# Opening of a hybrid mLSTM and pooling step: x transposed token tile by token tile, and four adaLN steps one chunk later

## The chip, the core and the metric

One core of a Trainium2 chip runs the kernel as one launch. The metric is the device time in microseconds, lower is better. The engines are TensorE (PE in the profile, with its weight loads as PEld), VectorE (DVE), ScalarE (ACT), GpSimd (POOL) and SyncE (SP), which here only issues transfers. Each engine works through its own list of instructions in order and waits on semaphores for the others. Every tile is float32.

## What is computed

One layer of a backbone over 384 tokens: 128 context tokens and 256 latent tokens, 2048 features each. Cut to what the opening works on:

```python
mod = jax.nn.silu(cond) @ ada_w + ada_b            # cond: c_ctx for the context, c for the latents
shift_a, scale_a, ... = mod reshaped to 6 x 2048
h = _rmsnorm(x, norm_w[0]) * (1 + scale_a) + shift_a
proj = h @ w_in                                    # q, k, v, o, gates, u
```

Behind that come a bidirectional mLSTM over q, k, v and a pooling mixer over u, one output projection, and an MLP of width 8192. They make up most of the time, and the change does not touch them.

## The kernel before, in words

Products are taken in three passes: each operand is split into a rounded high part (`hi`, made by ACT) and a remainder (`lo`, made by DVE), and PE adds hi·hi, hi·lo and lo·hi (line 503 for the stage at hand). Weights arrive in tiles named `raw_u`, `raw_v` and so on, which `load_w` (lines 122 to 142) loads through SP's queue and splits; three `raw` buffers go round.

The opening has these parts.

- **x.** The three token tiles `xtok` (128 tokens by 2048 features, 1 MB each) are loaded on SP's queue behind the two condition vectors `cc` and the constants `cst` (identity, ones, a selection matrix). ACT squares each tile and sums by token (line 389), and DVE and POOL make the reciprocal root `rx`. PE spreads it over all partitions (`bc_rx`), and DVE copies that to `rbc`.
- **Transposes.** The projections need the features on the partitions. `transpose_x(k)` takes one block of 128 features, transposes it for all three token tiles into one PSUM bank (line 403), and copies the 384 columns to `xT[k]`, on DVE for even k and on ACT for odd k (lines 409 to 411). So it needs all three tiles. The table `X_ORDER` orders the first eight blocks: "t" is one block, "a" one step of the adaLN generator, "b" the copy to `rbc`. Four more blocks come in `shift_rows`, between the two halves of `make_h(0)`, and the last four after the first weight chunk (`XT_AT`).
- **adaLN.** The modulation of two feature blocks (k-step of 256 features) at a time: PE multiplies the silu of both condition vectors by slabs `ada_raw` of ada_w (128x4x256, 512 KB, line 257), ACT copies the sum (`ada_sb`), PE turns it by small matmuls (line 273), and DVE adds the bias into `mod`. `first_ada` is a generator: each `next` does one slab or one later part. For features 0 to 255 it has two runs of four slabs (scale, then shift), ten steps in all. For features 256 to 511 it has eight slabs in a row, with the shift's four and then the scale's four; four buffers go round, so that the second four slabs may be loaded only when PE has read the first four. From features 512 on, `ada_eight` loads eight slabs at once, four of them into buffers that are free at the time (upper halves of the `u` tiles, which share memory with `xtok`, and part of `masks`; line 366).
- **The projection of u and v** (lines 491 to 526). Eight k-steps s, each with five weight chunks: u with 512 columns, u with 512, v with 3, 3 and 2 heads (the last with the gate columns). `make_h(s)` makes the modulated features `hm`, `hh`, `hl`. For s = 0, `ADA_STEPS` says how many adaLN steps PE does behind each chunk: four behind chunk 0 and four behind chunk 2. They are the eight slabs of features 256 to 511.

The order of PE, DVE and ACT is written by hand up to `order.close()` (line 488). From there PE's order is by hand up to the end of this loop; the other engines' lists, and SP's, are set by a scheduler.

Of the kernel before, what the change touches and what calls it, by code (L numbers as in the profile page):

```python
# [7 lines left out]
F32 = mybir.dt.float32  # L8
F32R = mybir.dt.float32r
AF = mybir.ActivationFunctionType  # L10
ALU = mybir.AluOpType
AX = mybir.AxisListType

P = 128
D = 2048
KT = D // P
NTOK = 384
# [10 lines left out]
N_W = 4  # L28
N_ADA = 4
N_E = 1  # L30
XT_AT = 0
ADA_STEPS = (4, 0, 4, 0, 0)
X_ORDER = "tatatatattaatabata"
N_X = 4
RATE_GF = 0.4
RATE_GS = 0.25
# [2 lines left out]
N_AHEAD = 3  # L39
# [5 lines left out]
def hymba_kernel(  # L45
# [6 lines left out]
    nc = tc.nc  # L52
    w_in, w_out, w1, w2, ada_w = w_in[0], w_out[0], w1[0], w2[0], ada_w[0]

    const = ctx.enter_context(tc.tile_pool(name="const", bufs=1))
    wp = ctx.enter_context(tc.tile_pool(name="wp", bufs=3))
# [4 lines left out]
    dram = ctx.enter_context(tc.tile_pool(name="dram", bufs=1, space=bass.MemoryType.DRAM))  # L61

    def slot(name, dt=F32):
        return slots.tile([P, 386], dt, tag="t", name=name)

    def bank(name):
        return psum.tile([P, 512], F32, tag="ps", name=name)


    cst = const.tile([P, 3, P], F32, name="cst")  # L70
    cs_src = consts.rearrange("p (n q) -> p n q", q=P)
    ident = cst[:, C_ID, :]
    ones = cst[:, C_ONE, :]
    cc = const.tile([P, 2, 16], F32, name="cc")
    vp_scope, pre_scope = ExitStack(), ExitStack()
    vp = vp_scope.enter_context(tc.tile_pool(name="vp", bufs=1))
    pre = pre_scope.enter_context(tc.tile_pool(name="pre", bufs=1))
    prm = pre.tile([P, 2, P], F32, name="prm")
    masks = vp.tile([P, N_CST - 3, P], F32, name="masks")
    nc.sync.dma_start(cc[:, 0, :], c_ctx.rearrange("(p j) -> p j", j=16))  # L80
    nc.sync.dma_start(cc[:, 1, :], c[0].rearrange("(p j) -> p j", j=16))
    nc.sync.dma_start(cst[:, 0:3], cs_src[:, 0:3])

    vsb = [vp.tile([P, NH, 129], F32, name=f"v{i}") for i in range(3)]
    gsb = vp.tile([P, 3, 32], F32, name="gsb")
    x_tok = [pre.tile([P, D], F32, tag=f"x{i}", name=f"xtok{i}") for i in range(3)]
    for t, src in zip(x_tok, (x_prompt[0], x_sample[0, 0:128], x_sample[0, 128:256])):
        nc.sync.dma_start(t, src)
    nc.gpsimd.dma_start(prm[0:96, 1, :], ada_b[0].rearrange("(r p) -> r p", p=P))
    nc.gpsimd.dma_start(prm[0:64, 0, :], norm_w[0].rearrange("i (k p) -> (i k) p", p=P))  # L90
    nc.gpsimd.dma_start(prm[64:72, 0, :], mlstm_norm_w[0].rearrange("(k p) -> k p", p=P))
# [106 lines left out]
    def rstd_cols(out, ss, n, scale):  # L198

        nc.vector.tensor_scalar(out, ss, scale, EPS, op0=ALU.mult, op1=ALU.add)  # L200
        nc.gpsimd.tensor_tensor(out, out, mhalf[:, 0:n], op=ALU.pow)
# [143 lines left out]
    def first_ada():  # L345
        for k0, nk in ksteps:
            if k0 == 0:
                yield from ada_mat([(1, k0, nk)])
                yield from ada_mat([(0, k0, nk)], ("lo",))
            elif k0 == 2:  # L350
                yield from ada_mat([(0, k0, nk), (1, k0, nk)])
            else:
                yield from ada_eight(k0)
# [21 lines left out]
        yield from ada_rows([(0, k0, 2), (1, k0, 2)], ps)  # L375

    ada0 = first_ada()
    pp = bank("pp")
    nc.tensor.transpose(pp[:, 0:96], prm[0:96, 1, :], ident[0:96, 0:96])
    nc.tensor.transpose(pp[:, 96:176], prm[0:80, 0, :], ident[0:80, 0:80])  # L380
    nc.vector.tensor_copy(prmT[:, 80:176], pp[:, 0:96])
    nc.vector.tensor_copy(prmT[:, 0:80], pp[:, 96:176])

    ssq = const.tile([P, 3, 2], F32, name="ssq")
    junk = wp.tile([P, 1024], F32, tag="hi", name="junk", bufs=N_W)
    rx = const.tile([P, 3], F32, name="rx")
    for i in (0, 1, 2):
        for q in range(2):
            nc.scalar.activation(junk, x_tok[i][:, q * 1024:(q + 1) * 1024], AF.Square, accum_out=ssq[:, i, q:q + 1])

    xT_dram = dram.tile([P, KT, NTOK], F32, name="xT_dram")
    xT = []
    rbc = pre.tile([P, NTOK], F32, name="rbc")
    ss = const.tile([P, 3], F32, name="ss")
    nc.vector.tensor_reduce(ss, ssq, axis=AX.X, op=ALU.add)
    rstd_cols(rx, ss, 3, 1.0 / D)

    xt_late = []

    def transpose_x(k, later=False):  # L400
        ps = bank(f"xt_{k}")
        for i in range(3):
            nc.tensor.transpose(ps[:, i * P:(i + 1) * P], x_tok[i][:, k * P:(k + 1) * P], ident)
        t = slot(f"xT{k}")
        xT.append(t)

        def copy():
            if k % 2:
                nc.scalar.activation(t[:, 0:NTOK], ps[:, 0:NTOK], AF.Copy)
            else:  # L410
                nc.vector.tensor_copy(t[:, 0:NTOK], ps[:, 0:NTOK])

        if later:
            xt_late.append(copy)
        else:
            copy()

    for op in X_ORDER:
        if op == "t":
            transpose_x(len(xT))  # L420
        elif op == "a":
            next(ada0)
        else:
            nc.vector.tensor_copy(rbc, bcast_row(rx, "rx")[:, 0:NTOK])
# [12 lines left out]
    def make_h(s, between=None):  # L437
        ts = []
        for k in range(ksteps[s][0], sum(ksteps[s])):
            t, hi, lo = slot(f"hm{k}"), slot(f"hh{k}", F32R), slot(f"hl{k}", F32R)  # L440
            ts.append((k, t, hi, lo))
            for g, (a, b) in enumerate(GROUPS):
                nc.vector.scalar_tensor_tensor(t[:, a:b], xT[k][:, a:b], mod[:, 1, k, g:g + 1], rbc[:, a:b], op0=ALU.mult, op1=ALU.mult)
        if between is not None:
            between()
        for k, t, hi, lo in ts:
            for g, (a, b) in enumerate(GROUPS):
                i1 = nc.scalar.activation(hi[:, a:b], t[:, a:b], AF.Identity, bias=mod[:, 0, k, g:g + 1])
                i2 = nc.vector.scalar_tensor_tensor(lo[:, a:b], t[:, a:b], mod[:, 0, k, g:g + 1], hi[:, a:b].bitcast(F32), op0=ALU.add, op1=ALU.subtract)
            h.append((hi, lo))  # L450
        return i1.ins, i2.ins
# [16 lines left out]
    def load_ahead(m, n):  # L468
        for q in range(m, min(m + n, NS * len(chunks))):
            if q not in loaded:  # L470
                s, ci = divmod(q, len(chunks))
                loaded[q] = load_chunk(s, ci, h_ins if s == 0 else ())
                if q == NS * len(chunks) - 1:
                    with tc.issue_after(load_w.ins):
                        nc.sync.dma_start(masks, cs_src[:, 3:N_CST])

    def shift_rows():
        for _ in range(2):
            transpose_x(len(xT), True)
        next(ada0)  # L480
        for _ in range(2):
            transpose_x(len(xT), True)

    h_ins = make_h(0, shift_rows)
    lo_later[0]()
    for copy in xt_late:
        copy()
    order.close()
    order2 = ExitStack()
    order2.enter_context(tc.manual_schedule(engines={mybir.EngineType.PE}))  # L490
    for s in range(NS):
        for ci, (kind, c0, w) in enumerate(chunks):
            k0, nk = ksteps[s]
            load_ahead(5 * s + ci, 1 if s + ci == 0 else N_AHEAD)
            hi, lo, n = loaded.pop(5 * s + ci)
            acc = [bank(f"{kind}_{c0}_{s}_{i}") for i in range(3)]

            ways = ((0, 0), (1, 0), (0, 1))
            for ps in [ways[n:n + 1] for n in range(3)] if s == ci == 0 else [ways]:
                for k in range(nk):  # L500
                    for i in range(3):
                        for a, b in ps:
                            nc.tensor.matmul(acc[i][:, 0:n], h[k0 + k][a][:, i * P:(i + 1) * P], (hi, lo)[b][:, k, :],  # L503
                                             start=k == 0 and a + b == 0, stop=k == nk - 1 and b == 1)
                    if ci == 3 and k == 0:
                        next(ada0, None)
            if s == ci == 0:
                load_ahead(1, 1)
            if s == 0 and ci == XT_AT:
                while len(xT) < KT:  # L510
                    transpose_x(len(xT))
            for _ in range((ADA_STEPS if s == 0 else (1, 1, 1, 0, 0))[ci]):
                next(ada0, None)
            if ci == 3 and s < NS - 1:
                make_h(s + 1)
            for i in range(3):
                if kind == "u":
                    dst, src = u_sb[i][:, c0:c0 + w], acc[i][:, 0:n]
                else:
                    dst, src = vsb[i][:, c0:c0 + w, 0:128], acc[i][:, 0:w * P].rearrange("p (h e) -> p h e", e=P)  # L520
                if s == 0:
                    nc.scalar.activation(dst, src, AF.Copy)
                else:
                    nc.vector.tensor_tensor(dst, src, dst, op=ALU.add)
                if kind == "v" and c0 == 6:
                    nc.vector.tensor_tensor(gsb[:, i, :], acc[i][:, w * P:n], gbias if s == 0 else gsb[:, i, :], op=ALU.add)
# [326 lines left out]
    ps = bank("ps_nout")  # L853
# [43 lines left out]
    for cols in ([0, 256], [512], [768], [1024], [1280], [1536], [1792]):  # L897
        if cols[0] in (768, 1024, 1280):
            for m in range(2):
                n = len(early)  # L900
                t = y[n // 2][:, 1024 * (n % 2):1024 * (n % 2) + 1024].rearrange("p (j c) -> p j c", c=256)
# [495 lines left out]
```

## Time and profile before

| | |
|---|---|
| Time, median of 3 runs | 1684.31 us (1683.07 to 1687.94) |
| Profiled execution, its own time | 1684.17 us |
| Its span from the first to the last instruction | 1682.5 us |
| Instructions | 27870 |
| Bytes moved by DMA | 320.95 MB, mean 191 GB/s |

Times in the profile count from the span's start. A row of the timeline gives start and length in us, engine, line, operation, tile written and tiles read, and in brackets the idle time ahead of it and what ended that. A row of the chain of waits gives start, length and what the chain went through. A row of the DMA view gives tiles, issuing queue, count, size and the median time from the start of the issue to landing. In a row of windows the last three numbers are the granted clock, the busy share of the DMA engines and GB/s.

### The profile page before, as it was taken

The numbers are of one execution on the slowest core, as the hardware profiler recorded it, in microseconds if no ns is written. First come the engines' busy times: TensorE is split into PE (matmuls) and PEld (weight loads), VectorE is DVE, ScalarE is ACT, GpSimd is POOL, SyncE is SP. The second block draws the span as 40 slices with busy tenths as digits, with TensorE's granted clock in tenths as the row PEclk, the third lists the DMA queues.
The fourth block names the chain that finished last, engine by engine and source line by source line (L and its number), as shares of the span: only waits on it lengthen the run. The fifth ranks groups of instructions, "written<-read, shape, count | busy, mean of one in ns | idle before, by whom it ended". The sixth has DMA issues, their size and how long they took to land.

```text
span 1682.5 us, 27870 instructions
## 1 busy us (share of the span) xinstructions
PE 1654.3 (98%) x10965; PEld 1581.4 (94%) x10965; DVE 1340.3 (80%) x2009; ACT 751.3 (45%) x1225; POOL 133.3 (8%) x185
## 2 busy tenths in 40 slices
PE   6999999999999999999999999999999999999997
PEld 3888999999999989989999999999999999999996
DVE  3677769898999959997897688988588588588688
ACT  5322355555443345543444444444444444445443
POOL 1000002221000024520000000000000000000120
PEclk9999999999999999999999999999999999999999
DMA  9999757786789954754546246444344443443653
GB/s 318 332 310 298 253 172 248 240 258 221 238 273 311 311 194 142 209 151 128 178 154 195 84 135 187 152 144 150 101 151 129 123 138 118 145 124 113 186 182 136
DMA packets 258099, 320.95 MB, mean 191 GB/s; under 512 B 14784, under 2 KB 223120, under 8 KB 257584
## 3 DMA queue, kind: packets, MB, share of 16 engines
q1 hardware_dynamic: 250688, 303.62, 57.1%
q0 software_dynamic: 5984, 13.78, 2.9%
q8 instruction: 86, 1.41, 0.4%
q10 hardware_dynamic: 1296, 1.77, 0.3%
q14 instruction: 45, 0.37, 0.1%
HBM read 308.61 MB, written 10.51 MB: 190 GB/s over the span
## 4 chain that ended last, share of the span: by engine, by line
PE 94%; DVE 3%; issue 1%; DMA 1%; ACT 0%; SPq 0%; POOL 0%; DVEq 0%; ACTq 0%; POOLq 0%
PE acc_w L145 10%; PE acc_w L144 10%; PE acc_w L146 10%; PE v L503 4%; PE y L1231 4%; PE y L1232 4%; PE y L1230 4%; PE u L503 4%; PE acc_wo L144 3%; PE acc_wo L145 3%; PE acc_wo L146 2%; PE y_yz L1231 2%; PE y_yz L1230 2%; PE y_yz L1232 2%; PE y L1074 2%; PE y L1073 2%
## 5 line engine op out<-in xcount | busy, mean ns | idle before, releaser
L145 PE MATMUL acc_w<-h2l,hi_w 128*128 128x384 f32 (+1 forms) x1024 | 346.2, 338 | 0.5 <-DVE h2l L1024 0.5
L144 PE MATMUL acc_w<-h2h,hi_w 128*128 128x384 f32 (+1 forms) x1024 | 344.2, 338 | 1.2 <-ACT h2h L1020 1.2
L146 PE MATMUL acc_w<-h2h,lo_w 128*128 128x384 f32 (+1 forms) x1024 | 345.1, 337 | 0.0
L136 DVE TENSOR_TENSOR lo_w<-raw_w,hi_w 128x1024 fp32r<-128x1024 f32 x152 | 185.3, 1220 | 136.5 <-ACT hi_w L135 136.3
L135 ACT ACTIVATE hi_w<-raw_w 128x1024 fp32r<-128x1024 f32 x152 | 160.8, 1058 | 213.7 <-PE acc_w L145 83.4
L317 DVE SCALAR_TENSOR_TENSOR ada_acc<-ada_raw,sg,ada_acc 128x1024 f32<-128x1024 f32 (+1 forms) x240 | 252.0, 1081 | 2.1 <-DMA ada_raw<-in_ada_w_dram 2.1
L144 PEld LDWEIGHTS acc_w<-h2h,hi_w 128*128 128x128 f32 x1024 | 192.2, 188 | 2.9 <-ACT h2h L1020 2.0
L145 PEld LDWEIGHTS acc_w<-h2l,hi_w 128*128 128x128 f32 x1024 | 192.6, 188 | 1.2 <-DVE h2l L1024 0.8
L146 PEld LDWEIGHTS acc_w<-h2h,lo_w 128*128 128x128 f32 x1024 | 192.4, 188 | 0.3 <-DVE lo_w L136 0.2
L1216 ACT ACTIVATE hi_t<-w 128x1024 fp32r<-128x1024 f32 x104 | 109.5, 1059 | 118.7 <-PE y L1232 34.0
L1217 DVE TENSOR_TENSOR lo_t<-w,hi_t 128x1024 fp32r<-128x1024 f32 x104 | 126.3, 1220 | 15.1 <-ACT hi_t L1216 14.7
L1217 DVE TENSOR_TENSOR lo_b<-w,hi_b 128x1024 fp32r<-128x1024 f32 x78 | 95.3, 1221 | 40.0 <-ACT hi_b L1216 39.8
L1216 ACT ACTIVATE hi_b<-w 128x1024 fp32r<-128x1024 f32 x78 | 82.5, 1060 | 97.0 <-PE acc_w L145 64.6
L135 ACT ACTIVATE hi_wo<-raw_wo 128x1024 fp32r<-128x1024 f32 x32 | 34.0, 1064 | 81.3 <-DMA raw_wo<-in_w_out_dram 64.0
L950 ACT ACTIVATE z<-acc_w 128x384 f32<-128x384 f32 x54 | 26.3, 487 | 74.8 <-PE acc_w L146 74.8
L503 PE MATMUL v<-hi_v,hh 128*128 128x384 f32 (+1 forms) x144 | 47.8, 332 | 0.0
L503 PE MATMUL v<-lo_v,hh 128*128 128x384 f32 (+1 forms) x144 | 46.5, 323 | 0.0
L503 PE MATMUL v<-hi_v,hl 128*128 128x384 f32 (+1 forms) x144 | 46.5, 323 | 0.0
L136 DVE TENSOR_TENSOR lo_wo<-raw_wo,hi_wo 128x1024 fp32r<-128x1024 f32 x32 | 38.8, 1218 | 7.3 <-ACT hi_wo L135 6.3
L986 POOL DMA_DIRECT2D gf_dram<-gfT x1 | 0.5, 521 | 551.9 <-DVE gfT L985 551.9
L144 PE MATMUL acc_k<-hh,hi_k 128*128 128x384 f32 x128 | 44.2, 345 | 0.0
L144 PE MATMUL acc_o<-hh,hi_o 128*128 128x384 f32 x128 | 43.9, 343 | 0.0
(2268 smaller groups left out, 4566.9 us busy)
## 6 DMA issues: line engine op xcount, KB each, us to landing
raw_w<-in_w_dram SPq DMA_DIRECT2D x152, 512.0 KB, 4.3
ada_raw<-in_ada_w_dram SPq DMA_DIRECT2D x130, 512.0 KB, 5.0
w<-in_w_dram SPq DMA_DIRECT2D x104, 512.0 KB, 4.4
raw_wo<-in_w_out_dram SPq DMA_DIRECT2D x32, 512.0 KB, 5.6
u<-in_ada_w_dram SPq DMA_DIRECT2D x18, 512.0 KB, 6.0
raw_u<-in_w_in_dram SPq DMA_DIRECT2D x16, 512.0 KB, 7.0
raw_q<-in_w_in_dram SPq DMA_DIRECT2D x16, 512.0 KB, 4.7
raw_k<-in_w_in_dram SPq DMA_DIRECT2D x16, 512.0 KB, 4.7
```

The lines of the kernel that those rows point to most:

```text
L135: nc.scalar.activation(hi[:, 0:n], raw[:, 0:n], AF.Copy)
L136: low = lambda: nc.vector.tensor_tensor(lo[:, 0:n], raw[:, 0:n], hi[:, 0:n].bitcast(F32), op=ALU.subtract)
L144: nc.tensor.matmul(ps, lh, rh, start=start, stop=False)
L145: nc.tensor.matmul(ps, lh, rl, start=False, stop=False)
L146: mm3.ins = nc.tensor.matmul(ps, ll, rh, start=False, stop=stop).ins
L317: nc.vector.scalar_tensor_tensor(acc[:, g, :], raw[:, a, :], cj, acc[:, g, :], op0=ALU.mult, op1=ALU.add)
L503: nc.tensor.matmul(acc[i][:, 0:n], h[k0 + k][a][:, i * P:(i + 1) * P], (hi, lo)[b][:, k, :], start=k == 0 and a + b == 0, stop=k == nk - 1 ...
L1216: nc.scalar.activation(hi, raw, AF.Copy)
L1217: nc.vector.tensor_tensor(lo, raw, hi.bitcast(F32), op=ALU.subtract)
L1230: nc.tensor.matmul(acc, xh, wh, start=start and j == 0, stop=False)
L1231: nc.tensor.matmul(acc, xh, wl, start=False, stop=False)
L1232: nc.tensor.matmul(acc, xl, wh, start=False, stop=stop and j == 3)
```

## The change

The three x tiles are transposed one after the other. Each has four PSUM banks of four blocks, and every block of 128 columns is copied on its own into its third of `xT[k]`; the last bank of the first tile and the last two banks of the third are copied by ACT, all others by DVE. All 48 transposes stand ahead of the first adaLN slab. The squares of a tile stand ahead of its transposes. The first x tile is the first transfer of SP's queue, `cc` follows, and `cst` goes out on ACT's queue. The eight adaLN steps of the first k-step stand four behind chunk 1 and four behind chunk 2, and the weights are loaded one chunk ahead for chunks 0 and 1.

```diff
-XT_AT = 0
-ADA_STEPS = (4, 0, 4, 0, 0)
-X_ORDER = "tatatatattaatabata"
+ADA_STEPS = (0, 4, 4, 0, 0)
+X_ORDER = "aaabaaaaaa"
...
-    nc.sync.dma_start(cc[:, 0, :], c_ctx.rearrange("(p j) -> p j", j=16))
-    nc.sync.dma_start(cc[:, 1, :], c[0].rearrange("(p j) -> p j", j=16))
-    nc.sync.dma_start(cst[:, 0:3], cs_src[:, 0:3])
+    nc.scalar.dma_start(cst[:, 0:3], cs_src[:, 0:3])
...
-    for t, src in zip(x_tok, (x_prompt[0], x_sample[0, 0:128], x_sample[0, 128:256])):
-        nc.sync.dma_start(t, src)
+    nc.sync.dma_start(x_tok[0], x_prompt[0])
+    nc.sync.dma_start(cc[:, 0, :], c_ctx.rearrange("(p j) -> p j", j=16))
+    nc.sync.dma_start(cc[:, 1, :], c[0].rearrange("(p j) -> p j", j=16))
+    for i in (1, 2):
+        nc.sync.dma_start(x_tok[i], x_sample[0, (i - 1) * P:i * P])
...
+    def transpose_x(i, k0, on_act):
+        ps = bank(f"xt_{i}_{k0}")
+        for a in range(4):
+            nc.tensor.transpose(ps[:, a * P:(a + 1) * P], x_tok[i][:, (k0 + a) * P:(k0 + a + 1) * P], ident)
+        for a in range(4):
+            dst, src = xT[k0 + a][:, i * P:(i + 1) * P], ps[:, a * P:(a + 1) * P]
+            if on_act:
+                nc.scalar.activation(dst, src, AF.Copy)
+            else:
+                nc.vector.tensor_copy(dst, src)
+
+    squares(0)
+    for q in range(4):
+        transpose_x(0, 4 * q, q == 3)
...
+    squares(1)
+    for q in range(4):
+        transpose_x(1, 4 * q, False)
+    squares(2)
+    for q in range(4):
+        if q == 2:
+            nc.vector.tensor_reduce(ss, ssq, axis=AX.X, op=ALU.add)
+            rstd_cols(rx, ss, 3, 1.0 / D)
+        transpose_x(2, 4 * q, q >= 2)
...
-    h_ins = make_h(0, shift_rows)
+    h_ins = make_h(0, lambda: next(ada0))
     lo_later[0]()
-    for copy in xt_late:
-        copy()
...
-            load_ahead(5 * s + ci, 1 if s + ci == 0 else N_AHEAD)
+            load_ahead(5 * s + ci, 1 if s == 0 and ci < 2 else N_AHEAD)
...
-            if s == 0 and ci == XT_AT:
-                while len(xT) < KT:
-                    transpose_x(len(xT))
```

The lists below give line, operation, tile written, tiles read, and the shape; "x4" is four in a row. The first is PE's list before, where u's chunk 0 (`u_0_0` to `u_0_2` with `hi_u_0_258`, `lo_u_0_259`) ends and chunk 1 (`hi_u_0_333`) begins:

```order
L503 MATMUL u_0_1_311<-lo_u_0_259,hh_267 128x512
L503 MATMUL u_0_2_312<-lo_u_0_259,hh_267 128x512
L403 MATMUL xt_337<-cst,xtok_89 128x128
...
L403 MATMUL xt_355<-cst,xtok_91 128x128
L257 MATMUL ada_2_361<-ada_raw_2_0_362,cT 32x256 x4
L257 MATMUL ada_2_361<-ada_raw_2_4_368,cT 32x256 x4
L257 MATMUL ada_2_361<-ada_raw_2_8_374,cT 32x256 x4
L257 MATMUL ada_2_361<-ada_raw_2_12_380,cT 32x256 x4
L503 MATMUL u_0_0_401<-hi_u_0_333,hh_262 128x512
```

Now PE's list from the end of chunk 1 (`hi_u_0_385`, `lo_u_0_386`) to v's first chunk (`hi_v_0_443`), and from its end to the second set of slabs:

```order
L493 MATMUL u_0_2_394<-lo_u_0_386,hh_343 128x512
L257 MATMUL ada_2_413<-ada_raw_2_0_414,cT 32x256 x4
L257 MATMUL ada_2_413<-ada_raw_2_4_420,cT 32x256 x4
L257 MATMUL ada_2_413<-ada_raw_2_8_426,cT 32x256 x4
L257 MATMUL ada_2_413<-ada_raw_2_12_432,cT 32x256 x4
L493 MATMUL v_0_0_460<-hi_v_0_443,hh_338 128x384
...
L493 MATMUL v_0_2_462<-lo_v_0_444,hh_343 128x384
L257 MATMUL ada_2_413<-ada_raw_2_0_481,cT 32x256 x4
L257 MATMUL ada_2_413<-ada_raw_2_4_487,cT 32x256 x4
L257 MATMUL ada_2_413<-ada_raw_2_8_493,cT 32x256 x4
L257 MATMUL ada_2_413<-ada_raw_2_12_499,cT 32x256 x4
```

The twelve transposes are gone from this place, the first set of slabs has moved behind chunk 1, and only v's first chunk is left between the two sets; before, chunk 1 and v's first chunk stood there.

SP's list now, from the last pieces of v's weights of the first k-step to the weights of the second (`u_326` is the spare half of a u tile):

```order
L129 DMA raw_v_0_453<-in_w_in_dram 128x2x256
L129 DMA raw_v_0_453<-in_w_in_dram 128x2x32
L366 DMA u_326<-in_ada_w_dram 128x4x256
L253 DMA ada_raw_2_0_481<-in_ada_w_dram 128x4x256
L253 DMA ada_raw_2_4_487<-in_ada_w_dram 128x4x256
L253 DMA ada_raw_2_8_493<-in_ada_w_dram 128x4x256
L253 DMA ada_raw_2_12_499<-in_ada_w_dram 128x4x256
L129 DMA raw_u_1_510<-in_w_in_dram 128x2x512
L129 DMA raw_u_1_563<-in_w_in_dram 128x2x512
```

The load of `u_326` is new at this place: before, it stood behind the weights `raw_u_1` and the next `raw_v`, and the second set of slabs followed the `raw_v_0` pieces directly. Apart from this one and the first rows, where `xtok` now precedes `cc` and `cst` is gone, SP's list has the same order as before.

More of the change, by code (lines that the diff above doesn't have):

```diff
@@ L377, in hymba_kernel, with squares @@
     ada0 = first_ada()
+    ssq = const.tile([P, 3, 2], F32, name="ssq")
+    junk = wp.tile([P, 1024], F32, tag="hi", name="junk", bufs=N_W)
+    rx = const.tile([P, 3], F32, name="rx")
+    ss = const.tile([P, 3], F32, name="ss")
+    xT_dram = dram.tile([P, KT, NTOK], F32, name="xT_dram")
+    xT = [slot(f"xT{k}") for k in range(KT)]
+    rbc = pre.tile([P, NTOK], F32, name="rbc")
+    def squares(i):
+        for q in range(2):
+            nc.scalar.activation(junk, x_tok[i][:, q * 1024:(q + 1) * 1024], AF.Square, accum_out=ssq[:, i, q:q + 1])
+    def transpose_x(i, k0, on_act):
[11 more added lines that the diff above has]
+        transpose_x(0, 4 * q, q == 3)
     pp = bank("pp")
@@ L382, in hymba_kernel @@
     nc.vector.tensor_copy(prmT[:, 0:80], pp[:, 96:176])
[L384 to L415, printed above, removed]
-            copy()
+    squares(1)
[7 more added lines that the diff above has]
+        transpose_x(2, 4 * q, q >= 2)
     for op in X_ORDER:
-        if op == "t":
-            transpose_x(len(xT))
-        elif op == "a":
+        if op == "a":
             next(ada0)
@@ L475, in load_ahead @@
                         nc.sync.dma_start(masks, cs_src[:, 3:N_CST])
[L477 to L482, printed above, removed]
-    h_ins = make_h(0, shift_rows)
+    h_ins = make_h(0, lambda: next(ada0))
     lo_later[0]()
-    for copy in xt_late:
-        copy()
     order.close()
@@ L508, in hymba_kernel @@
                 load_ahead(1, 1)
-            if s == 0 and ci == XT_AT:
-                while len(xT) < KT:
-                    transpose_x(len(xT))
             for _ in range((ADA_STEPS if s == 0 else (1, 1, 1, 0, 0))[ci]):
```

## The prediction

> **What bounds the kernel now.** I read the page's busy shares first, then TensorE's waits from 30 us to the end, then the chain of the opening, then the transfers that the chain rests on.
>
> ```profile
> PE 1654.3 (98%) x10965; PEld 1581.4 (94%) x10965; DVE 1340.3 (80%) x2009; ACT 751.3 (45%) x1225; POOL 133.3 (8%) x185
> PE   6999999999999999999999999999999999999997
> PE acc_w L144 <- ACT h2h L1020: 1.2, 2, 0.7
> ```
>
> TensorE (PE) is busy 98% of the span, and only the first of the 40 slices is far from full. The last row is the largest of the six entries in PE's waits from 30 us to the end; together they are 3.7 us in 1650. So PE's own work sets the end from 30 us on. A change of the opening is worth the time by which PE gets earlier or later through the first projection weights, and nothing later gives it back or adds to it, unless a new wait appears. The chain of the opening, start, length, what:
>
> ```profile
> 16.32 1.08 PE ada L257 x8
> ...
> 21.50 0.57 PE ada L257 x8
> ...
> 28.03 0.39 ACT ada_sb L269
> 28.42 0.95 ACT hi_u L135
> ...
> 29.39 0.41 ACT hh L448
> ...
> 29.84 4.61 PE u L503 x18
> 34.45 1.31 PE xt L403 x12
> 35.76 1.86 PE ada L257 x32
> 37.62 4.38 PE u L503 x18
> 42.01 3.16 PE v L503 x18
> 45.17 1.87 PE ada L257 x32
> 47.03 1.78 PE v L503 x9
> ```
>
> From 29.84 us PE does, without a gap: u chunk 0, twelve transposes, four adaLN slabs (x32: 2 passes of 16), u chunk 1, v chunk 0, four more slabs, v chunk 1. All seven pieces must be done in any order; I follow the start of v chunk 1, 47.03 us, because behind it PE's list of work is the same in both kernels. Before 29.84 the transfers set the pace. Here each transfer has its issue row and then its row of the DMA view, whose last number is the time from issue to landing:
>
> ```profile
> 0.81 0.38 SPq L80 DMA_DIRECT2D cc<-in_c_ctx_dram  x1
> 2.18 0.43 SPq L88 DMA_DIRECT2D xtok<-in_x_prompt_dram  x1
> xtok<-in_x_prompt_dram SPq DMA_DIRECT2D x1, 1024.0 KB, 5.5
> 17.85 1.42 SPq L253 DMA_DIRECT2D ada_raw<-in_ada_w_dram  x1
> ada_raw<-in_ada_w_dram SPq DMA_DIRECT2D x1, 512.0 KB, 8.9
> 19.31 1.41 SPq L129 DMA_DIRECT2D raw_u<-in_w_in_dram  x1
> raw_u<-in_w_in_dram SPq DMA_DIRECT2D x1, 512.0 KB, 8.8
> 20.00:24.00 4.00, 4.00 (x41) 2.24 (x40) 1.44 (x4) 1.37 (x3) 0.00 (x0) 1.00 1.10 348
> ```
>
> The eighth slab lands at 17.85 + 8.9 = 26.75, the first weights raw_u at 19.31 + 8.8 = 28.1. The queue runs full at 348 GB/s (last row, last column), or 1.51 us for 512 KB. hi_u starts 0.3 us after its data, so the start of u is tied to the transfer stream and not to the transposes.
>
> **The change part by part.** *x first.* The first x tile moves from the fourth place of SP's queue (issue 2.18) to the first (0.81): at most 1.37 us earlier, at least nothing. cst goes to ACT's queue, but its bytes and those of cc still have to be carried, and 208 KB at 348 GB/s are 0.6 us, which leaves 0.8. The queue was not yet full in those first microseconds, so I take 1.0. Then raw_u lands at 27.1, the eighth slab at 25.75; its matmuls (0.57) and copy (0.39) are over by 26.8. From raw_u: hi_u 1.05, and from its end to the first u matmul as before 29.84 - 29.37 = 0.47. u starts at **28.6**, 1.2 earlier.
>
> *Transposes.* All 48 stand ahead of the slabs, while PE waits for transfers. The twelve that stood behind u chunk 0 leave the chain: **1.31** less. A gain of 2.5 us so far. The cover: x's first tile lands near 6.7 (2.18 + 5.5 - 1.0), the first slab near 15.3, and u starts at 28.6. In these 22 us PE has 48 transposes, 5.2 us at 1.31 / 12 or twice that at a slow clock, and eight slabs of 0.57 to 1.08, so 10 to 19 us of work.
>
> *Copies.* Each token tile is copied out in 16 pieces of 128 columns, 48 in all (DVE 36, ACT 12), where there were 16 of 384. None of this shape is in the trace. The nearest:
>
> ```profile
> 9.26 0.26 DVE L381 COPY prmT<-pp 128x96 f32<-128x96 f32 x1 [3.45 <-PE pp L380]
> 20.12 0.56 DVE L411 COPY xT<-xt 128x384 f32<-128x384 f32 x1 [2.16 <-PE xt L403]
> ```
>
> Between 0.26 and 0.56 each; 0.29 by a straight line between the DVE rows, and near the lower one. DVE's eight for the last tile are then 2.3 us, over by about 18, and rx and rbc, which wait behind them, are needed only some 9 us later: nothing on the path. At 0.56 the 36 take 20 us, rbc comes at about 28 and u would start some 2 us later; that is the upper end. The six squares on ACT keep their number, and the issue of cst there (0.4, as on SP) comes ahead of a table load that waits for cc anyway.
>
> *cc behind x.* The silu chain and the clearing of cT were ready near 6 us; behind 1 MB of x they come about 4 us later, still 5 ahead of the first slab. No cost. ACT now splits v's first weights after u chunk 1's second bank instead of ahead of the bank copies; at the 1.05 of hi_u or less it lies under the 1.86 of the first slab set.
>
> *The four slabs one chunk later.* This makes a new wait. The second set of four slabs uses the buffers of the first set, so SP can issue them only as PE reads the first set. Issue and landing before, first and last of the second set:
>
> ```profile
> 36.39 0.37 SPq L253 DMA_DIRECT2D ada_raw<-in_ada_w_dram  x1
> ada_raw<-in_ada_w_dram SPq DMA_DIRECT2D x1, 512.0 KB, 4.0
> 37.95 0.46 SPq L253 DMA_DIRECT2D ada_raw<-in_ada_w_dram  x1
> ada_raw<-in_ada_w_dram SPq DMA_DIRECT2D x1, 512.0 KB, 7.6
> ```
>
> Counted from PE's start on the first set (35.76), the second set lands at +4.6 to +9.8. PE needed its last slab at 45.17 + 3/4 of 1.87 = 46.57, +10.8: one microsecond to spare. u chunk 1, 4.38 us, stood between the two sets and now stands ahead of both. PE reaches the first set at 28.6 + 4.61 + 4.38 = 37.6 and the last slab of the second at 37.6 + 1.86 + 3.16 + 1.40 = 44.0, +6.4. If the second set lands as before, its last slab comes at 37.6 + 9.8 = 47.4 and PE waits 3.4 us; if the four follow each other at 1.51, at 37.6 + 4.6 + 4.5 = 46.7, a wait of 2.7. The queue has drained by then, and one more transfer of 512 KB (for u's spare half) stands in front of the set, so it cannot go ahead of PE. After the last slab (0.47) v chunk 1 starts at 47.2 to 47.9.
>
> *Sum.* 47.03 becomes 47.2 to 47.9: +0.2 to +0.85, I take +0.5. The gain of 2.5 is spent in the new wait. The profiled execution took 1684.17 us, with a span of 1682.5, and 0.14 less than the median of the three runs, 1684.31. The forecast is 1684.17 + 0.5 = **1684.7**.
>
> **The rivals.** *Cold array (slower).* PE had a slow state in the opening that the granted clock (1.00 throughout) doesn't show:
>
> ```profile
> 20.01 1.01 PE L257 MATMUL ada<-ada_raw,cT 128*32 128x256 f32 x8
> 21.43 0.64 PE L257 MATMUL ada<-ada_raw,cT 128*32 128x256 f32 x8
> ```
>
> In the chain the same eight passes cost 1.08 at 16.32 and 0.57 from 21.50 on, after 4 to 5 us without a gap. Before, PE kept busy until u because the transposes filled the gaps between slabs. Now it works 0.57 of every 1.5 us for ten microseconds ahead of u. If that lets it fall back, the eighteen matmuls of u chunk 0 begin slowly: over 4.6 us the loss is 4.6 x (1 - 0.57/1.08) = 2.2 us, and everything behind moves with it: 1686.9. It decides from the share of idle time at which the array slows down. No stretch of this trace has PE fast and then two thirds idle, so the rows speak neither way; as each gap is only about a microsecond, I give it 0.25. [...]
>
> *No new wait.* The second set lands by +6.4 and the gain stays: 1684.17 - 2.5 = 1681.7. Against it: a single slab took 4.0 from issue, and the fourth is issued over 2 us after PE's start. 0.08.
>
> *x is not earlier.* POOL's small transfers or the copies hold the stream, u starts at 29.8: 1685.9. 0.06.
>
> *Late weights of the next k-step.* The raw_u pair of k-step 1 stands behind the second set.
>
> ```profile
> 40.15 0.37 SPq L129 DMA_DIRECT2D raw_u<-in_w_in_dram  x1
> raw_u<-in_w_in_dram SPq DMA_DIRECT2D x1, 512.0 KB, 9.5
> 50.21 1.05 ACT L135 ACTIVATE hi_u<-raw_u 128x1024 fp32r<-128x1024 f32 x1
> 51.53 1.49 ACT L448 ACTIVATE hh<-hm,mod 128x128 fp32r<-128x128 f32 x4
> ```
>
> Its second landed at 49.65, hi_u started 0.56 later, and hh was ready 1.3 ahead of PE's need at 53.2 (47.03 + 1.78 + 0.34 + 4.05): 1.8 us of cover. It should land 1.6 to 1.9 later while PE is 0.2 to 0.85 later, so the cover holds by a few tenths. Each microsecond beyond is one of PE's; two of them give 1686.7, and only some five would pass 0.3%. 0.05.
>
> **How the numbers follow.** Forecast 0.56 (1683.7 to 1685.7), cold array 0.25 (1686 to 1688), no wait 0.08, x not earlier 0.06, late weights 0.05. From 1681.7 to 1688.0 these leave out less than 2 in 10, with the dearest copies inside. 0.3% of this kernel is 5 us, about what a measurement can tell from no change. No case reaches it alone: faster 0.01; slower 0.03, if cold array and late weights come together; within 0.96.
>
> **What would show it.** u's first matmul near 28.6; the chain of 29 to 35 without transposes; an idle stretch of 2.7 to 3.4 us on PE before or among the second four slabs, ended by the ada_raw transfer, in SP's order behind PE's reads; v chunk 1 near 47.5. u chunk 0 taking 6 us or more would show the cold array; a PE wait for hh near 53 the late weights. Wrong altogether if PE has no wait there, or if the span moves by over 4 us.

## The result and the profile after

| | before | after |
|---|---|---|
| Median of 10 runs | 1684.29 us (1683.07 to 1687.94) | 1688.83 us (1687.42 to 1691.79) |
| Ratio after / before, 95% interval | | 1.0027 (1.0017 to 1.0037) |
| Profiled execution, span | 1684.17, 1682.5 us | 1689.48, 1687.8 us |

The change costs 4.5 us, 0.27%, where 0.4 us were forecast. The chain of the kernel after, from the transfer of the first weights on (start, length, what):

```profile
18.69 9.47 DMA raw_u<-in_w_in_dram
...
28.18 1.06 ACT hi_u L135
...
29.59 10.48 PE u L493 x36
40.07 1.91 PE ada L257 x32
...
42.26 7.68 DMA ada_raw<-in_ada_w_dram
...
49.99 0.64 PE ada L257 x8
50.63 3.07 PE v L493 x9
53.69 0.61 PE ada L273 x4
54.30 4.06 PE v L493 x27
58.36 8.36 PE u L493 x36
```

The same pieces stand here as in the chain before, without the transposes. Both u chunks are one row now, 10.48 us instead of 4.61 + 4.38 = 8.99. A transfer stands in the middle of the chain, and behind it `v x9` takes 3.07 us instead of 1.78. u of k-step 1, the last row, begins at 58.36; before it began at 47.03 + 1.78 + 0.34 + 4.05 = 53.2. That is 5.15 us, and PE stays about that much behind until the end (span +5.3).

TensorE's wait for slabs from 25 to 60 us in the kernel after (us in total, times, longest), SP's issue of the second set, and that set on TensorE's timeline (in brackets the idle time ahead and what ended it):

```profile
PE ada L257 <- DMA ada_raw<-in_ada_w_dram: 4.6, 5, 1.1
```

```profile
40.70 2.02 SPq L253 DMA_DIRECT2D ada_raw<-in_ada_w_dram  x4
```

```profile
45.23 0.64 PE L257 MATMUL ada<-ada_raw,cT 128*32 128x256 f32 x8
46.76 0.64 PE L257 MATMUL ada<-ada_raw,cT 128*32 128x256 f32 x8 [0.89 <-DMA ada_raw<-in_ada_w_dram]
48.53 0.64 PE L257 MATMUL ada<-ada_raw,cT 128*32 128x256 f32 x8 [1.14 <-DMA ada_raw<-in_ada_w_dram]
49.99 0.64 PE L257 MATMUL ada<-ada_raw,cT 128*32 128x256 f32 x8 [0.81 <-DMA ada_raw<-in_ada_w_dram]
```

SP issues the set only behind PE's start on the first set (40.07). The last three slabs arrive 1.5 to 1.8 us apart, and the last lands at 42.26 + 7.68 = 49.94, 9.87 behind that start. PE needed it at 45.23 + 1.40 = 46.63 and got it at 49.99, 3.4 us later: 2.8 are the three waits in brackets (the other two of the five lie ahead of u), and the rest is that each slab on its own takes 0.64 us instead of the 0.47 of a slab within four. The load of `u_326`, which stands in front of the set in SP's list, had no part in it: it was issued at 34.37 and landed 5.4 us later, before 40.70.

The slow stretches are in the granted clock. These are windows of the kernel after; the columns used here are the stretch, its length, PE's busy time, and, third from the end, the granted clock:

```profile
19.99:23.40 3.41, 2.72 (x30) 1.07 (x29) 1.41 (x5) 0.38 (x1) 0.00 (x0) 1.00 1.10 348
23.40:26.82 3.42, 1.64 (x24) 0.32 (x16) 0.87 (x3) 0.00 (x0) 0.00 (x0) 1.00 1.07 371
26.82:30.23 3.41, 1.66 (x6) 1.47 (x7) 0.78 (x3) 2.43 (x6) 0.00 (x0) 0.50 1.08 356
30.23:33.64 3.41, 3.41 (x10) 2.67 (x10) 3.18 (x5) 1.34 (x2) 0.00 (x0) 0.50 1.10 349
33.64:37.06 3.42, 3.42 (x16) 2.79 (x15) 0.00 (x0) 1.58 (x3) 0.00 (x0) 1.00 1.02 315
...
47.30:50.71 3.41, 1.46 (x21) 0.47 (x18) 0.00 (x0) 0.02 (x1) 0.00 (x0) 1.00 1.07 379
50.71:54.12 3.41, 3.41 (x13) 3.41 (x13) 0.00 (x0) 1.42 (x2) 0.00 (x0) 0.50 1.07 365
```

Read them in pairs. In 23.40 to 26.82 PE is busy 1.64 of 3.42 us, and the clock of the next window is 0.50. It stays there until a window is full (30.23 to 33.64), and the one behind that is back at 1.00. In 47.30 to 50.71, while PE waits for slabs, it is busy 0.43 of the time, and the next window, with `v x9` in it, is slow. A full window at 0.50 does 1.7 us less work, an estimate (half of 3.41). The bounds aren't chosen here: in this trace every change of the clock falls on this grid of 3.41 us. (Before, the clock read 1.00 even while eight passes cost 1.08 at 16.32; its record begins at 20.83 us, between the slabs of 0.94 at 20.08 and 0.57 at 21.50, so that slow start isn't in it.)

### The profile page after: what moved, and what is told of

It is laid out like the page before. It is cut to its first block, busy times and chain, and to the rows that moved or that the text cites. A ratio compares the mean times of both kernels' runs of the same rounds, so it can differ in the third digit from the quotient of the medians.

```text
span 1687.8 us, 27905 instructions
## 1 busy us (share of the span) xinstructions
PE 1658.9 (98%) x10965; PEld 1587.8 (94%) x10965; DVE 1342.6 (80%) x2037; ACT 749.2 (44%) x1229; POOL 132.1 (8%) x185
## 4 chain that ended last, share of the span: by engine, by line
PE 87%; DVE 6%; DMA 3%; issue 2%; SPq 1%; ACT 1%; POOL 0%; DVEq 0%; ACTq 0%; POOLq 0%
PE acc_w L144 9%; PE acc_w L145 9%; PE acc_w L146 9%; PE v L493 4%; PE u L493 4%; PE y L1218 4%; PE y L1219 4%; PE y L1217 4%; PE acc_wo L144 3%; PE acc_wo L145 2%; PE acc_wo L146 2%; PE y_yz L1218 2%; PE y_yz L1217 2%; PE y_yz L1219 2%; PE y L1059 2%
## 5 line engine op out<-in xcount | busy, mean ns | idle before, releaser
L144 PE MATMUL acc_q<-hh,hi_q 128*128 128x384 f32 x128 | 43.9, 343 | 0.0
```

Source lines behind the costliest of these rows:

```text
L144: nc.tensor.matmul(ps, lh, rh, start=start, stop=False)
```

## The experiments

Times below are medians of 5 to 11 runs, with the ratio to the kernel before on the same chip and its 95% interval. The number to compare in the opening is the start of u of k-step 1: 53.2 before, 58.36 after.

**e1: the steps back.** The kernel after with

```diff
-ADA_STEPS = (0, 4, 4, 0, 0)
+ADA_STEPS = (4, 0, 4, 0, 0)
```

> The kernel after, with the eight adaLN steps at their old places (four behind chunk 0, four behind chunk 2); x, transposes, copies and transfers as in the kernel after. Theory A (the loss comes from the four slabs moved one chunk later: 3.6 us of wait for the second slab set and 1.6 us of a slow array behind it): no wait of PE for ada_raw behind 30 us, `v x9` at 1.8 us instead of 3.07, v chunk 1 at 46.0 to 47.8 instead of 50.63, the time 3.5 to 5 us under the kernel after, within 1 us of the kernel before. u chunk 0 still begins slowly (about 6 us), since the slabs ahead of it come as in the kernel after. Rival B (the loss comes from the transposes and the slow array ahead of u alone): the time stays at least 2.5 us over the kernel before.

1686.07 us, 1.0002 (0.9993 to 1.0011). Its chain:

```profile
29.97 6.77 PE u L493 x18
36.74 1.86 PE ada L257 x32
...
46.15 1.86 PE ada L257 x32
48.02 1.78 PE v L493 x9
...
54.19 8.36 PE u L493 x36
```

The second set has no wait, `v x9` is at full speed, and 4.2 of the 5.15 us are gone. u chunk 0 still takes 6.77 us, more than in the kernel after, since the clock was at 0.50 for three windows here (24.86 to 35.10). v chunk 1, 48.02, is 0.2 later than the theory's bound for that reason.

**e2: the steps alone.** The kernel before with

```diff
-ADA_STEPS = (4, 0, 4, 0, 0)
+ADA_STEPS = (0, 4, 4, 0, 0)
```

> The kernel before, with only the adaLN steps moved (four behind chunk 1, four behind chunk 2); x, transposes, copies and transfers as before. Theory A: PE reaches the first set at 34.45 + 1.31 + 4.38 = 40.1, the second set lands up to +9.9 behind that, at 50.0, v chunk 1 starts near 50.5 and, if gaps of 1 us make the array slow, takes 1.3 us more: the time 3.5 to 5.2 us over the kernel before, as much as the whole change. u chunk 0 stays at 4.6 us. Rival B: no wait or one under 1 us, the time within 1 us of the kernel before.

1691.36 us, 1.0037 (1.0025 to 1.0050): 6.0 us over the kernel before, at least as much as the whole change, where 3.5 to 5.2 were expected. Its chain:

```profile
30.44 4.61 PE u L503 x18
35.05 1.31 PE xt L403 x12
...
40.55 1.91 PE ada L257 x32
...
42.74 9.20 DMA ada_raw<-in_ada_w_dram
...
51.98 1.08 PE ada L257 x8
53.06 3.18 PE v L503 x9
```

u begins at full speed, so the transposes between the slabs did keep the clock up; the last slab lands 11.4 us behind PE's start on the first set, and two slow windows follow the wait (49.78 to 56.60). The 11.4 hold more than the gate: the scheduler changed SP's list too, and here the two loads of `raw_u` for k-step 1 (issued at 36.86 and 39.88) stand in front of the set (41.18). So the wait is shown by e2, but its size isn't that of the moved steps alone. With e1, where the wait goes with the steps, this puts the loss on the moved steps.

**e4 and e5: work for PE in the gaps.** Eight transposes of constants, into a bank that nobody reads, behind each slab of k-step 0 (e4) or behind the first three of the second set of k-step 1 (e5):

```diff
+                fill = 8 if k0 == 0 else 0 if b == 1 and j0 < 12 else 0   # e4
+                fill = 0 if k0 == 0 else 8 if b == 1 and j0 < 12 else 0   # e5
+                if fill:
+                    wps = bank(f"fill_{i}_{k0}_{j0}")
+                for _ in range(fill):
+                    nc.tensor.transpose(wps[:, 0:P], cst[:, C_ONE, :], ident)
```

> The kernel after, with eight transposes of constants added behind each of the first eight slabs, into a bank that nobody reads; the rest as in the kernel after. They fill about 0.9 us of each 1.5 us between slabs. If gaps of about 1 us at 40% load made the array slow ahead of u: u chunks 0 and 1 take 9.0 to 9.3 us instead of 10.48, v chunk 1 comes 1.2 to 1.5 earlier than 50.63, and the time is 1.2 to 1.5 us under the kernel after. If something else slowed u chunk 0 (its operands, the copies of xT, the transfers): u chunks 0 and 1 stay at 10.4.

> The kernel after, with eight transposes of constants added behind each of the first three slabs of the second set of k-step 1, where PE waits for the next slab; the rest as in the kernel after. If the gaps made the array slow there: the wait for the last slab stays (v chunk 1 near 50.6), but `v x9` takes 1.8 us instead of 3.07 and the small matmuls 0.34 instead of 0.61, and the time is about 1.5 us under the kernel after. If the slow v chunk 1 has another cause: `v x9` stays near 3 us and the time that of the kernel after.

The edit also hit a later adaLN stage that runs the same lines (from 612 us on in the kernel before; 32 transposes more in e4, 24 in e5), so their whole times, 1693.56 and 1695.49 us, don't measure the opening. The chains do, e4's row first, then e5's:

```profile
30.85 8.81 PE u L498 x36
```

```profile
50.18 0.57 PE ada L257 x8
50.75 1.78 PE v L498 x9
...
56.93 8.36 PE u L498 x36
```

Both slow stretches went where PE was kept at work, and nothing else was changed: 8.81 instead of 10.48, 1.78 instead of 3.07. Of the gain at u, e4 kept only 0.6 us (u of k-step 1 at 57.75), since its u began 1.3 later: slab and eight transposes take 0.57 + 1.02 us, more than the 1.5 between two slabs.

**e6: both, in the opening alone.**

> The kernel after, with eight transposes of constants (nobody reads them) behind each of the eight slabs of k-step 0 and behind the first three slabs of the second set of k-step 1, and nowhere else in the program. Theory A (the granted clock falls to 0.50 where PE is short of work for some microseconds): clock 1.00 from 18 to 60 us, u chunks 0 and 1 in 8.8 to 9.2 us, `v x9` 1.8; but the second set still lands near +9.8 from PE's start on the first, so v chunk 1 starts near 50.2 and u of k-step 1 near 56.3 instead of 58.36: the time about 2 us under the kernel after, so still over the kernel before by about 2.5. Rival (the slow stretches come from something else than missing work, and stay): the time of the kernel after or more.

1689.54 us, 1.0018 (1.0009 to 1.0027), 3.7 us over the kernel before, with no stretch at 0.50 in the opening. u of k-step 1 stands at 56.99, 1.4 before the kernel after; 2 were expected (the eight transposes behind the last slab are on the path, and u started at 31.07). So even at full clock the wait keeps this order behind the kernel before.

**e9: six slab buffers.** The kernel after with

```diff
-N_SLOT = 55
+N_SLOT = 50
-N_ADA = 4
+N_ADA = 6
```

> The kernel after, with six adaLN slab buffers instead of four (and 50 instead of 55 slots to make room; the order of u_326 and raw_u of k-step 1 on SP's queue changes with it). Two slabs of the second set then need not wait until PE has read the first set. Theory A (the wait is the buffer gate): these two land before PE needs them, the last lands by 46.5, PE's wait for ada_raw behind 40 us falls from 3.5 to under 1.2 us, `v x9` takes 1.8, u of k-step 1 starts at 53.3 to 54.2 instead of 58.36. The slow start of u stays, about 10.5 for chunks 0 and 1. Rival (the stream itself is late, not the gate): last slab near 50, wait 3 us or more, u of k-step 1 at 57 or later.

Its chain, and a row of PE's waits behind 25 us:

```profile
39.11 1.86 PE ada L257 x32
40.97 3.33 PE v L493 x18
44.31 1.86 PE ada L257 x32
46.17 1.78 PE v L493 x9
...
52.34 8.40 PE u L493 x36
```

```profile
PE acc_w L146 <- DVE lo_w L136: 3.9, 1, 3.9
```

With two slabs free of the gate there is no wait at all at the second set, and u of k-step 1 starts 6.0 us earlier than in the kernel after. So the gate is the wait. (The order of SP's list changed as well, with `u_326` now behind `raw_u` of k-step 1; but in the kernel after `u_326` had landed before the set was issued, as shown above, so that isn't the cause.) The kernel as a whole is slower, 1691.47 us, 1.0030 (1.0019 to 1.0041), with PE's wait of 3.9 us for `lo_w` in it. Why the smaller slot pool does that wasn't pursued.

**e10: the first set in the lo tiles' buffers,** a second way around the gate:

```diff
-yield from ada_mat([(0, k0, nk), (1, k0, nk)])
+yield from ada_mat([(0, k0, nk), (1, k0, nk)], ("lo", "ada"))
```

> The kernel after, with the first set of k-step 1's slabs in the four buffers of the lo tiles (as the second run of k-step 0 has them) and the second set in the slabs' own four, so that no slab of the second set waits for PE's read of the first; the memory stays as it is, the order of the slabs and of v's weights on SP's queue changes. Theory A (the wait is the buffer gate): no PE wait for the second set, no granted clock of 0.50 between 45 and 60 us, u of k-step 1 at 52.5 to 54.2 instead of 58.36, the time 4 to 5.5 us under the kernel after, unless lo tiles that come later make PE wait for lo_u or lo_v (then that wait shows by name). Rival: u of k-step 1 at 57 or later.

1689.77 us, 1.0028 (1.0019 to 1.0037), a miss. In the chain the second set goes without a wait, but the first set has one now:

```profile
29.61 11.34 PE u L493 x36
...
40.97 3.55 DMA ada_raw<-in_ada_w_dram
...
45.20 4.91 PE v L493 x18
50.11 1.86 PE ada L257 x32
...
58.16 8.74 PE u L493 x36
```

The order of SP's queue changed with the buffers, and a slab of the first set lands at 44.5. A slow stretch follows: `v x18` takes 4.91 us, where e1 has 3.16. The wait was moved, not removed.

**e11: x fourth again.** e1 with `cc`, `cst` and the first x tile issued in the old order on SP's queue.

> The kernel after, with the adaLN steps at their old places and with cc, cst and the first x tile issued in the old order on SP's queue (x fourth). Only the token-wise transposes and copies and the load-ahead are left of the change. If x first were worth the 1.0 us that was forecast: raw_u lands about 1 us later than in the run with the steps back (28.55), the time 1 us over it. If it is worth nothing, as eight runs with x first suggest (raw_u at 27.05 to 28.55, mean 27.9, against 28.09 and 27.85 with x fourth): raw_u lands at 27.5 to 28.5 and the time is within 1 us of the run with the steps back.

1686.97 us, 1.0007 (0.9998 to 1.0016), 0.9 over e1; u starts at 29.85, in e1 at 29.97. The landings of raw_u that the expectation lists show no lead (mean 27.9 where x is first, 28.09 and 27.85 where it is fourth). The traces of after and before hold sixteen marks for the landing of each load, and these tell where the lead goes. The first x tile lands at 6.78 after, where it is first, and at 7.66 before, where it is fourth. The eighth slab lands at 26.08 and 26.73. raw_u's first mark comes at 25.60 and 26.29, and its fifteenth at 27.41 and 28.03. Only the last, which `hi_u` waits for, is no earlier (28.16 and 28.09): it comes 0.75 after the fifteenth where x is first and 0.06 where it is fourth. What holds up this last part stays open.

**e12 and e13: both kernels again.**

> The kernel before, unchanged, for a second profile. Theory (the clock is set by windows of 3.41 us whose place differs from run to run): another place of the windows, no stretch at 0.50 in the opening, since PE is busy at least 0.84 of any such window from 17 to 60 us; a stretch of 3.41 us at 0.50 near 541 if a window covers most of the small matmuls and the wait from 538.5 to 541.1, none otherwise. u of k-step 1 within 0.7 us of 53.21. The ratio holds 1.000.

> The kernel after, unchanged, for a second profile. Theory: the wait for the second set is there again (v chunk 1 at 50 to 51.5), and one or two windows at 0.50 behind it, one to three around the start of u, at other places than in the first profile; their number times 1.7 us is the difference in u chunks 0 and 1 and in v chunk 1. Rival (slow stretches fixed to the instruction, not to windows): the same nine matmuls of u and the same nine of v are slow.

Before again: 1685.58 us, 1.0002 (0.9994 to 1.0011). Its opening repeats (u of k-step 1 at 53.20), but its profiled span is 1685.1, 2.6 over that of the first profile. About 1.7 of this, by the estimate above for a full window at 0.50, come near 541 us, where every one of the kernels has this on PE (timeline of the first profile):

```profile
538.48 0.95 PE L273 MATMUL ada_gate<-cst,ada_sb 128*128 128x4 f32 x8
540.17 1.05 PE L336 MATMUL adaf<-cst,adav_sb 128*128 128x4 f32 x8 [0.75 <-ACT adav_sb L332]
```

Windows there in the first profile of before and then in the second:

```profile
539.66:543.07 3.41, 2.90 (x19) 2.90 (x20) 3.41 (x9) 1.22 (x3) 0.00 (x0) 1.00 1.06 376
543.07:546.48 3.41, 3.41 (x22) 3.41 (x21) 3.41 (x8) 1.43 (x5) 0.00 (x0) 1.00 1.09 352
```

```profile
540.19:543.61 3.42, 2.67 (x20) 2.59 (x20) 3.42 (x7) 1.46 (x4) 0.00 (x0) 1.00 1.07 374
543.61:547.02 3.41, 3.41 (x13) 3.41 (x12) 3.21 (x7) 1.43 (x5) 0.00 (x0) 0.50 1.07 366
```

Nothing was changed between the two, but the grid lies elsewhere against the work: in the first profile the window holds 1.6 us of the 2.7 us of small matmuls and wait, and 0.51 of the wait of 0.75; in the second the whole wait lies in it (2.67 of 3.42 busy), and there the next one is slow. e1, e7 and e8 have such a window at 0.50 as well. The first profiles of before and after don't, so their spans can be compared without it.

After again: 1689.56 us, 1.0025 (1.0016 to 1.0033). The first set starts at 39.98, the last slab lands at 49.54 (+9.6), u chunks 0 and 1 take 10.02 and `v x9` 3.18 us. The clock is at 0.50 from 26.18 to 33.00 and from 50.07 to 53.48. The grid lay only 0.64 us off the first profile's, so this pair tells little about whether the slow stretch follows the window; e1 with its three slow windows and the pair around 541 tell it.

**e7, e15, e16: the steps back and filling work.** e1 with five transposes of constants behind each of the first seven slabs; e15 and e16 are the same kernel, for more profiles.

> The kernel after, with the adaLN steps at their old places and five transposes of constants (nobody reads them) behind each of the first seven slabs of k-step 0. Theory A: no wait for slabs behind 30 us and no stretch of granted clock under 1.00; u starts at 29.3 to 29.9, the chain to v chunk 1 is 4.4 + 1.87 + 4.38 + 3.16 + 1.87 = 15.7, so v chunk 1 at 45.0 to 45.6 (before 47.03): the time 1.2 to 2.0 us under the kernel before. That is what x first and the moved transposes are worth by themselves. Rival (the gain is lost elsewhere, as by other waits later): within 0.5 us of the kernel before, or above it.

> The same kernel as e7_back_fill, for a second profile: its profiled run gained 2.1 us in the opening, its median run nothing. Either the opening varies (u of k-step 1 at 52 to 54 here, with a window at 0.50 in the opening or a later raw_u), or the opening is as in the first profile (51.1 to 51.6) and the time is given back behind it, by windows at 0.50 or waits behind 60 us.

> The same kernel once more, for a third profile: as for the second, either u of k-step 1 is at 52 to 54, or at 51.1 to 51.6 with later losses.

The last rows of the opening's chain in e7:

```profile
44.93 1.78 PE v L498 x9
...
51.11 8.36 PE u L498 x36
```

u of k-step 1 starts at 51.11, 52.19 and 51.42 in the three profiles, 1.0 to 2.1 us earlier than before; u chunk 0 takes 6.18 us in e15 and 4.63 in e16. Behind the opening, e7 has a window at 0.50 from 539.36 to 542.76 and small waits (0.8 for `r2bc`, 1.1 for `lo_b`); the spans are 1683.1, 1683.4 and 1683.6. The median of e7 is 1687.14 us, 1.0007 (0.9998 to 1.0016): no gain. The three profiled runs (1684.83, and 1685.12 and 1685.35 on another chip) are among the shortest of this kernel, and what its longer ones lose, no profile here shows.

**e8 and e14: the kernel's own transposes as filling work.** e1 with the last 16 or 24 transposes of x held back and put between the slabs of k-step 0 (each "t" is four; the lines that hold them back aren't shown):

```diff
-X_ORDER = "aaabaaaaaa"
+X_ORDER = "aaabaaatatatat"      # e8
+X_ORDER = "aaabaaattattatat"    # e14
```

> The kernel after, with the adaLN steps at their old places and the third x tile's sixteen transposes held back: four behind each of the last four slabs of k-step 0, work that has to be done anyway. Theory A: PE has about 0.5 + 0.45 us of work per 1.5 us there, the clock stays at 1.00 or falls later than in the run with the steps back alone; u chunk 0 at 4.4 to 5.5 us instead of 6.77, v chunk 1 at 45.2 to 46.7, the time 0.5 to 1.8 us under the kernel before. Rival (two thirds of load aren't enough to hold the clock): u chunk 0 over 6 us, the time within 1 us of the kernel before or over it.

> The kernel after, with the adaLN steps at their old places and 24 transposes held back: the second x tile's last eight and the third's sixteen, behind the last six slabs of k-step 0 in groups of 4, 4, 8, 4, 4 (work that has to be done anyway). If the share of busy time in each window of 3.41 us decides, PE is at 0.75 or more in each window from 20 to 30 us, the clock stays at 1.00 or falls at most for the window that holds the wait for hh, u chunk 0 takes 4.4 to 5.0 us or once 6.1, v chunk 1 starts at 45.3 to 47.0. The time is then between 2 us under the kernel before and equal to it. Rival (held-back transposes delay xT and so hm): u starts after 30.5.

e8: 1685.67 us, 0.9997 (0.9989 to 1.0006); u chunk 0 takes 6.11 us, since the window 26.83 to 30.25 was busy 0.56 (the wait for hh lies in it) and the next one is slow. That is the rival's outcome, but not for its reason: the window before, with the slabs, was busy 0.81 and held the clock. e14: 1687.90 us, 1.0008 (0.9999 to 1.0017), u at 32.32, a miss, and the rival's outcome. Its windows:

```profile
12.69:16.11 3.42, 0.97 (x11) 0.28 (x9) 1.84 (x10) 3.33 (x7) 0.00 (x0) 1.00 1.06 358
16.11:19.52 3.41, 2.44 (x17) 0.75 (x18) 0.89 (x3) 0.58 (x2) 0.89 (x1) 0.50 1.09 349
19.52:22.93 3.41, 2.91 (x13) 0.95 (x12) 0.56 (x1) 0.38 (x1) 0.00 (x0) 0.50 1.10 349
```

Work held back for later gaps emptied an earlier window (0.97 of 3.42), and the clock was low until 26.35. No version beat the kernel before.

## Why the prediction was wrong

The forecast of v chunk 1 at 47.2 to 47.9 became 50.63, and behind it 1.6 us more were lost.

| step | forecast | kernel after |
|---|---|---|
| u starts | 28.6 | 29.59 |
| u chunks 0 and 1 | 4.61 + 4.38 = 8.99 | 10.48 |
| last slab behind PE's need | 2.7 to 3.4 | 3.4 |
| `v x9` and the small matmuls | 1.78 + 0.34 | 3.07 + 0.61 |

*The four slabs one chunk later* was right in mechanism and size: the gate, +9.8 from PE's start on the first set (9.87 and 9.6), the wait of 3.4 us. e2 shows it with x and the transposes as before (longer there, behind two loads of `raw_u`), and e9 shows it go.

*Cold array* is the step that failed. The sum took u chunks 0 and 1, v chunk 1 and the small matmuls at full speed, so a slow array stood in it at nothing; it was left to a rival at 0.25, because "each gap is only about a microsecond". Gaps of that length were enough: between 23.40 and 26.82 PE's longest is 0.88, its busy time 1.64 of 3.42, and the next window is at 0.50. What e1, e4, e5 and e8 agree on is the share of busy time in a window of 3.41 us. The rows that the rival quoted give the share, 0.57 of work per 1.51 us, which is 0.38; that this is too little no row of before could tell. The slow state that it saw beside a granted clock of 1.00 stood ahead of that clock's record, which starts only at 20.83; in e2 the same eight passes cost 1.08 again, at 51.98, inside a stretch at 0.50. Its price for u, 2.2, was near (1.5). But its place was asked after only once: the wait that the forecast itself added leaves PE busy 0.43 of a window, and so costs 1.6 behind its end as well. The forecast gave the wait its length and nothing for what follows it.

*x first*, 1.2 us at the start of u, was worth 0.25. The tile did land 0.9 earlier (6.78 for 7.66), but raw_u didn't (28.16 for 28.09), and the landings in e11's expectation say the same. The forecast was near for fifteen of the sixteen parts of that load, which keep a lead of 0.4 to 0.8 us; the last part loses it, and the sum had no term for that. So the outcome of one more rival (*x is not earlier*, 0.06) came together with the cold array, while the chances add up to 1.00 as if only one could come. These 1.0, with 1.5 for u and 1.6 for v, are the 4.1 us by which the sum with a wait of 3.4 (+0.85) falls short of +5.15, to 0.2.

*Transposes* left the chain as forecast (1.31). *Copies* took 0.28 us each on DVE (0.29 forecast) and nothing waited for them. *Late weights* did not come: in the chain u of k-step 1 follows v's last chunk without a gap (`raw_u`'s second load landed at 53.07, 3.4 us later than before, and PE came to it 5.15 us later). The forecast that nothing behind the opening adds or gives back held for the kernel after, but e7 and e12 show that it holds to a few microseconds only.

## What to carry to other kernels

Before moving work out of a gap on TensorE, cut its timeline into windows of 3.41 us and ask which of them are left short of work: in the opening of this kernel windows busy 0.56 or less were followed by one at 0.50, which cost up to 1.7 us, and the new wait brought such a window with it (busy 0.43). Where a load reuses a buffer that an engine still reads, the distance from that read to the next need must hold the whole landing time of the set, here 9.6 to 9.9 us for four slabs; putting work ahead of the read doesn't lengthen that distance. Differences of 0.1% need a second profile of the unchanged kernel, since the same kernel's span moved by 2.6 us.

## What the runs showed of the hardware

In the traces of before and after each stretch of granted clock between its first and last change is a whole number of windows of 3.41 us (3, 2, 5, 1 and 477 in after, 485 in before), and so is each stretch at 0.50 that e1, e2, e4, e5, e7, e8 and e9 show whole, one to three of them. The grid lies differently from run to run: the first slow window begins at 26.82 in after, 26.18 in e13 and 24.86 in e1. Between 10 and 60 us, these windows at 1.00 were followed by one at 0.50: busy 0.48 and 0.43 in after, 0.44 and 0.33 in e13, 0.28 in e14, 0.56 in e8, and, from rows of 1 us, about 0.50 in e1, 0.45 in e5 and in e9, 0.33 in e2 and 0.32 in e4. In the two of after the longest gap was 0.88 and 1.14 us. Windows busy 0.80 and 0.74 in after (from 19.99 and 43.88) and 0.81 in e8 were followed by 1.00. The way back took more: windows busy 0.72 and 0.85 (e14, above) stayed at 0.50, one busy about 0.92 (e9, from 28.78) and the full ones of after (from 30.23 and 50.71) were followed by 1.00. Near 541 us the busy share alone doesn't decide: a window busy 0.78 was followed by 0.50 in e1, e7, e8 and e12, and by 1.00 in after (542.23 to 545.64). What differs is how much of the 2.7 us of small matmuls and wait lies in the window: by the rows of 1 us all of it in e1, e7 and e8, 1.7 us in after, and 1.6 in the first profile of before, which kept 1.00 too. Why that should count, no run here shows.
